# A hybrid decoder step on one core: cached keys laid out feature-major on the host, key transposes taken out

## The chip, the cores and the metric

The kernel runs on one core of one Trainium2 chip. The metric is the device time of one execution in microseconds (us).

## What is computed

One layer for 256 prompt tokens and 32 sample tokens (8 sequences of 4), 288 tokens together: a modulated RMSNorm, one input projection, three token mixers (a spatial gMLP, a gated DeltaNet, a sparse attention), one output projection. The change is in the sparse attention of the sample tokens, which looks at 2048 cached keys per sequence, held in 16 pages of 128 keys with 2 heads of 128 features:

```python
idx, valid = _indexer_topk(q_idx, w_idx, pos, kidx_all, top_k)        # 256 of 2052 keys per query
k_sel = jnp.where(is_past, cache_k[phys, off], _gather_rows(k, nidx))
v_sel = jnp.where(is_past, cache_v[phys, off], _gather_rows(v, nidx))
s = jnp.einsum('bthgd,btkhd->bthgk', q, k_sel) * C_HEAD ** -0.5
p = jax.nn.softmax(jnp.where(valid, s, -jnp.inf), axis=-1)
```

The kernel scores all cached keys and masks those that were not selected.

## The kernel before

**Order of work.** A planner (class Weaver) writes the program. Units of matrix product (tile `acc`: weight matrices split in two parts, 12 matmuls of 288 columns for each half of a 512 KB weight load) are listed by hand; between the steps of a unit, generators (the attention, the DeltaNet, and so on) put in their own stages whenever the planner's clock says that their inputs are there. So most stages are covered by `acc` matmuls, and each engine runs its instructions in the order in which the planner wrote them. The planner's clock uses costs of its own: 1.0 us of GpSimd for each DMA that GpSimd issues (line 193), 0.003 + 0.000416 us per column for an `acc` matmul, which is 0.123 us (line 119), and for data that GpSimd gathers 0.6 us, the bytes at 360 GB/s and 2.0 us until they can be read (lines 193 to 206).

**Forced waits.** `W.finish(...)` runs named generators to their end without any `acc` matmul between them. Before the last unit of each q, k or v group of the DeltaNet projection stands `end_prev` (lines 2285 to 2290): all causal convolutions (`CONV`) that have been started must be finished, and for the third q group (g = 2, kind 0) also `DN[0]`, the first of the four DeltaNet head groups. `DN[0]` starts when the sample attention is done (`X.g_smp.done`, line 1701).

**The sample attention.** `idx_sample_gen` builds gather indices from the page table, gathers and scores the indexer keys, sets `idx_done`, and goes on with `topk_gen`: 32 rounds of max and replace on VectorE, each followed by a small copy `LDn<-LU` on GpSimd. `sample_gen` runs in two halves `hf` of 4 sequences. In each half:

- 16 gathers of keys into `kraw` (two buffers). One gather fetches 128 rows of 4 KB, one per partition: 4 neighbouring keys, 2 heads, 128 features; 512 KB.
- two lanes, `qk_lane(0)` and `qk_lane(1)`, take them in turn. For each gather there are 8 transposes on TensorE into two PSUM banks (tile `kT`), two copies out of them (VectorE and ScalarE, tile `ktk`), 8 score matmuls for 32 query rows each (tile `S`, each of which is two instructions in the trace), and two copies of scores by ScalarE into `S`.
- then gathers of values (tile `vraw`, 2 KB rows, buffers shared with `kraw` and `kt`), the mask matmuls once top-k is done (`X.topk`), softmax, transposes `pT`, value matmuls `so`.

The gathers are indirect DMAs, issued from GpSimd's queue. In the same queue stand the `LDn` copies, the constants `Rm` and `segm`, and the convolution taps of the sample tokens (`cv`, `tap`, `SSG`). Every kernel instruction is recorded at line 74, the wrapper of the engines, so the views are read by tile names.

Of the kernel before, what the change touches and what calls it, by code (L numbers as in the profile page):

```python
# [12 lines left out]
I32 = mybir.dt.int32  # L13
# [6 lines left out]
P = 128  # L20
# [70 lines left out]
class Weaver:  # L91
# [195 lines left out]
    def bank(self, n=1):  # L287

        yield
        while not self.room(n):  # L290
            yield lambda: self.room(n)
        self.take(n)
# [88 lines left out]
def tile_hybrid_step(ctx: ExitStack, tc: tile.TileContext, I, O):  # L381
# [22 lines left out]
    def tl(pool, shape, name, bufs=1, dt=F32, tag=None):  # L404
        return W.tile(pools[pool][1], shape, dt, tag or name, name, bufs)
# [764 lines left out]
    def idx_sample_gen():  # L1170
# [4 lines left out]
        dma(ptB, bass.AP(tensor=pt.tensor, offset=pt.offset, ap=[[0, P], [1, P]]))  # L1175
        iof = tl("ap", [P, 16], "iof")
        G.iota(iof, pattern=[[1, 16]], base=0, channel_multiplier=0, allow_small_or_imprecise_dtypes=True)
        sub16 = tl("ap", [P, 1], "sub16")
        V.memset(sub16, 0.0)
        sv = tl("ap", [P, 4], "sv")  # L1180
        V.memset(sv, 16.0)

        for q in range(4):
            G.affine_select(sv[:, q:q + 1], sv[:, q:q + 1], pattern=[[0, 1]], compare_op=OP.is_ge, fill=0.0,
                            base=-32 * q - 16, channel_multiplier=1)
            G.affine_select(sv[:, q:q + 1], sv[:, q:q + 1], pattern=[[0, 1]], compare_op=OP.is_ge, fill=0.0,
                            base=32 * q + 31, channel_multiplier=-1)
        iop = tl("ap", [P, 2], "iop")
        G.iota(iop[:, 0:1], pattern=[[0, 1]], base=0, channel_multiplier=1, allow_small_or_imprecise_dtypes=True)
        m15 = tl("ap", [P, 16], "m15")  # L1190
# [3 lines left out]
        V.scalar_tensor_tensor(iop[:, 1:2], iop[:, 1:2], -8.0, iop[:, 0:1], op0=OP.mult, op1=OP.add)  # L1194
        V.tensor_scalar(iop[:, 1:2], iop[:, 1:2], 8.0, None, op0=OP.mult)

        ptm = pts[:, 384:448].rearrange("p (b j) -> p b j", j=16)
        G.memset(ptm, 0.0)
        for u in range(2):
            G.affine_select(ptm, ptm, pattern=[[-32, 4], [-1, 16]], compare_op=OP.not_equal, fill=1.0,  # L1200
                            base=-16 * u, channel_multiplier=1)
        ptj = pts[:, 448:464]
        G.affine_select(ptj, ones[:, 0:16], pattern=[[-8, 16]], compare_op=OP.is_ge, fill=0.0, base=0,
                        channel_multiplier=1)
        G.affine_select(ptj, ptj, pattern=[[8, 16]], compare_op=OP.is_ge, fill=0.0, base=7, channel_multiplier=-1)
        yield [ptB]
        V.tensor_reduce(sub16, sv, axis=AX.X, op=OP.max)
        ptf = tl("ap", [P, 3], "ptf")
        ptvf = tl("ap", [P, NB], "ptvf")
        V.tensor_copy(ptF, ptB)  # L1210
        V.tensor_tensor(ptT, ptF, ident, op=OP.mult)
        V.tensor_reduce(ptf[:, 0:1], ptT, axis=AX.X, op=OP.add)
        V.tensor_tensor(ptT.rearrange("p (h n) -> p h n", h=2), ptF.rearrange("p (h n) -> p h n", h=2),
                        pts[:, 384:448][:, None].to_broadcast([P, 2, 64]), op=OP.mult)
        V.tensor_reduce(ptf[:, 1:3], ptT.rearrange("p (h n) -> p h n", h=2), axis=AX.X, op=OP.add)
        V.tensor_tensor(ptT.rearrange("p (b j) -> p b j", j=16), ptF.rearrange("p (b j) -> p b j", j=16),
                        ptj[:, None].to_broadcast([P, NB, 16]), op=OP.mult)
        V.tensor_reduce(ptvf, ptT.rearrange("p (b j) -> p b j", j=16), axis=AX.X, op=OP.add)
        ix8 = tl("ap", [P, 8], "ix8", 1, I32)
        V.scalar_tensor_tensor(ix8, ptf[:, 0:1].to_broadcast([P, 8]), 8.0, iof[:, 0:8], op0=OP.mult, op1=OP.add)  # L1220
        X.ixk = tl("ap", [P, 2, 16], "ixk", 1, I32)
        for hf in range(2):
            V.tensor_scalar(ptf[:, 1 + hf:2 + hf], ptf[:, 1 + hf:2 + hf], 32.0, sub16, op0=OP.mult, op1=OP.add)
            V.tensor_scalar(X.ixk[:, hf], iof, ptf[:, 1 + hf:2 + hf], None, op0=OP.add)

        V.tensor_scalar(ptvf, ptvf, 64.0, iop[:, 1:2], op0=OP.mult, op1=OP.add)
        X.ixv = tl("ap", [P, NB, 8], "ixv", 1, I32)
# [203 lines left out]

    def sample_gen():
        yield lambda: hasattr(X, "qready")
        k_rows = I["cache_k"][0].rearrange("n (e l) h d -> (n e) (l h d)", e=32)
        v_rows = I["cache_v"][0].rearrange("n (e l) h d -> (n e) (l h d)", e=64)
        qS = X.qS
        yield lambda: hasattr(X, "idx_done")
        def gather_k(hf, s):
            raw = tl("ap", [P, 4, 256], "kraw", 2)
            G.indirect_dma_start(out=raw.rearrange("p l c -> p (l c)"), out_offset=None, in_=k_rows,  # L1440
                                 in_offset=bass.IndirectOffsetOnAxis(ap=X.ixk[:, hf, s:s + 1], axis=0))
            return raw

        def gather_v(hf, s):
# [14 lines left out]
        for hf in range(2):  # L1459

            S = tl("ap", [P, NK], "S", 1, tag="S")
            Sk = S[:, 0:2048].rearrange("p (c k) -> p c k", k=P)
            raws = [gather_k(hf, 0), gather_k(hf, 1)]

            def qk_lane(par):
                raw = raws[par]
                for s in range(par, 16, 2):
                    yield [raw]
                    yield from bank(2)
                    pk = [pr4("kT") for _ in range(2)]  # L1470
                    for kv in range(2):
                        for l in range(4):
                            T.transpose(pk[kv][:, l], raw[:, l, kv * HD:(kv + 1) * HD], ident)
                    if s + 2 < 16:
                        raw = gather_k(hf, s + 2)
                    yield [pk[1]]
                    kt = tl("ap", [P, 2, 4, P], "ktk", 2, tag="kt")
                    V.tensor_copy(kt[:, 0], pk[0])
                    A.copy(kt[:, 1], pk[1])
                    free(2)  # L1480
                    yield from bank()
                    ps = pr("S")
                    qk_mm(ps, P, hf, lambda kv, bb: kt[:, kv, :, 32 * bb:32 * bb + 32])
                    yield
                    dst = Sk[:, 4 * (s % 4):4 * (s % 4) + 4].rearrange("p l (j u w) -> p l w u j", u=2, w=4)[:, :, s // 4]
                    for u in range(2):
                        A.activation(dst[:, :, u], ps[:, 0:P].rearrange("p (l u j) -> p u l j", l=4, u=2)[:, u], AF.Copy,
                                     scale=HD ** -0.5)
                    free()

            ls = W.push(qk_lane(0), qk_lane(1), front=True)
            yield lambda: all(x.done for x in ls)
            raws = []
            raws += list(gather_v(hf, 0)) + list(gather_v(hf, 1))
            yield from bank()
# [921 lines left out]
    for i, (_, n, t0) in enumerate(xsrc):  # L2417
# [11 lines left out]
    close_pool("fp")  # L2429


_INS = ["x_prompt", "x_sample", "cache_k", "cache_v", "cache_kidx", "state_dn", "state_conv", "page_table",
        "c_prompt", "c_sample", "w_ada_t", "b_ada", "g_norm", "w_in_t", "w_in_c", "a_vnorm", "a_ws", "a_bs", "dn_conv_w",
        "dn_a_log", "dn_dt_bias", "dn_onorm", "w_out_t", "g_final"]
_OUTS = [((1, 256, 4096), "float32"), ((8, 4, 4096), "float32"),
# [6 lines left out]
def lay_out(inputs):  # L2442

    import numpy as np

    a = dict(inputs)
    w = np.asarray(a.pop("w_in"))[0]
    idx = np.concatenate([np.arange(c, c + 512) for c in GCOL])
    a["w_in_t"] = w[:, idx].reshape(16, 2, P, 29, 512).transpose(3, 0, 2, 1, 4)
    c = np.concatenate([w[:, C_KIWI:C_KIWI + 80], w[:, C_AB:C_AB + 32]], axis=1)  # L2450
    a["w_in_c"] = c.reshape(16, 2, P, 112).transpose(0, 2, 1, 3)
    a["w_out_t"] = np.asarray(a.pop("w_out"))[0].reshape(16, 2, P, 8, 512).transpose(3, 0, 2, 1, 4)
    w = np.asarray(a.pop("w_ada"))[0]
    blocks = []
    for k0, n in STEPS:
        x = w[:, :2 * D].reshape(n * 8, 4 // n, P, 2, D)[..., k0 * P:(k0 + n) * P]
        blocks.append(x.transpose(0, 2, 1, 3, 4).reshape(8 * n, P, 1024))
    for f in range(4):
        blocks.append(w[:, 2 * D + 1024 * f:2 * D + 1024 * f + 1024].reshape(KT, P, 1024))
    a["w_ada_t"] = np.concatenate(blocks)  # L2460
    return a
# [21 lines left out]
```

## Time and profile before

| | |
|---|---|
| median of 3 runs | 2645.76 us (2639.38 to 2648.55) |
| the profiled execution | 2644.57 us, span 2642.8 us |
| TensorE (PE) busy | 2531.5 us, 96% of the span |
| VectorE (DVE), ScalarE (ACT), GpSimd (POOL) busy | 62%, 40%, 19% |
| mean granted TensorE clock | 0.986 of full |

Matmuls overlap in the records, so a busy TensorE is not one at its peak; what one matmul costs is read from the distance between starts, and from the chain.

### The profile page before, as it was taken

How to read it: one execution, taken by the hardware profiler on the slowest of the kernel's cores; microseconds unless marked ns; L12 is line 12 of the kernel's file. 1: busy time of each engine (PE TensorE's matmuls, PEld its weight loads, DVE VectorE, ACT ScalarE, POOL GpSimd, SP SyncE). 2: the span in 40 equal slices, each digit the busy share in tenths (PEclk: the TensorE clock that was granted, in tenths of full speed). 3: DMA queues.
4: the chain of work that ended last, by engine and by line, in shares of the span. 5: the costliest groups of instructions: out<-in, count | busy, mean ns of one | idle time of the engine just before them, and what ended most of it. 6: DMA issues, size and time to landing. Idle time of an engine off the chain costs nothing.

```text
span 2642.8 us, 52171 instructions
## 1 busy us (share of the span) xinstructions
PE 2531.5 (96%) x19684; PEld 2237.9 (85%) x19684; DVE 1629.5 (62%) x3633; ACT 1064.3 (40%) x2440; POOL 495.5 (19%) x1137
## 2 busy tenths in 40 slices
PE   5999999999998999999999989999999999999997
PEld 2777878888897878877789969989989989999997
DVE  3377765555567777744457658568576667555554
ACT  3433233323244443334254444444444544444443
POOL 1000000000001042263542333443440210000000
PEclk9999999999999999999999999999999999999998
DMA  7998988888656477677767547567568465655564
GB/s 276 339 326 327 346 320 301 313 312 302 239 171 209 162 236 239 207 278 251 255 221 248 173 147 245 179 212 255 178 202 267 146 193 183 179 181 177 175 187 164
DMA packets 234964, 615.91 MB, mean 233 GB/s; under 512 B 38856, under 2 KB 92348, under 8 KB 234712
## 3 DMA queue, kind: packets, MB, share of 16 engines
q1 hardware_dynamic: 223672, 574.65, 64.6%
q0 software_dynamic: 11040, 37.92, 4.2%
q8 instruction: 155, 2.54, 0.4%
q14 instruction: 97, 0.79, 0.1%
HBM read 587.54 MB, written 24.95 MB: 232 GB/s over the span
## 4 chain that ended last, share of the span: by engine, by line
PE 85%; DMA 6%; DVE 3%; issue 2%; POOL 2%; ACT 1%; SPq 0%; another core or an unknown queue 0%; ACTq 0%; DVEq 0%; POOLq 0%
PE acc L74 68%; PE ada L74 7%; DMA kraw<-in_cache_k_dram,ixk 2%; DMA wa<-in_w_ada_t_dram 1%; PE Sup L74 1%; PE kT L74 1%; PE YP L74 1%; DVE wl L74 1%; DMA w<-in_w_in_t_dram 1%; PE v L74 1%; PE so L74 1%; PE gram L74 1%; PE o L74 1%; DMA prev<-in_state_conv_dram 0%; DMA vraw<-in_cache_v_dram,ixv 0%
## 5 line engine op out<-in xcount | busy, mean ns | idle before, releaser
L74 DVE TENSOR_TENSOR wl<-w,wh 128x512 fp32r<-128x512 f32 (+1 forms) x1216 | 803.0, 682 | 694.9 <-ACT wh L74 645.1
L74 ACT CAST wh<-w 128x512 fp32r<-128x512 f32 (+1 forms) x1216 | 714.3, 611 | 1173.3 <-PE acc L74 846.0
L74 PE MATMUL acc<-hH,wh 128*128 128x288 f32 (+1 forms) x3744 | 1159.7, 310 | 14.4 <-ACT hH L74 8.7
L74 PE MATMUL acc<-hH,wl 128*128 128x288 f32 (+1 forms) x3744 | 1108.7, 296 | 6.0 <-DVE wl L74 3.9
L74 PE MATMUL acc<-hL,wh 128*128 128x288 f32 (+1 forms) x3744 | 1107.8, 296 | 1.3 <-issue 0.9
L74 PEld LDWEIGHTS acc<-hH,wh 128*128 128x128 f32 (+1 forms) x3744 | 706.4, 189 | 175.6 <-ACT wh L74 90.2
L74 PEld LDWEIGHTS acc<-hH,wl 128*128 128x128 f32 (+1 forms) x3744 | 706.9, 189 | 9.7 <-DVE wl L74 7.6
L74 PEld LDWEIGHTS acc<-hL,wh 128*128 128x128 f32 (+1 forms) x3744 | 707.4, 189 | 4.4 <-issue 3.2
L74 PE MATMUL acc<-mL,wh 128*128 128x288 f32 x1024 | 302.4, 295 | 2.5 <-DVE mL L74 2.5
L74 PE MATMUL acc<-mH,wh 128*128 128x288 f32 x1024 | 304.3, 297 | 0.0
L74 PE MATMUL acc<-mH,wl 128*128 128x288 f32 x1024 | 302.8, 296 | 0.0
L74 PEld LDWEIGHTS acc<-mL,wh 128*128 128x128 f32 x1024 | 193.0, 188 | 2.7 <-DVE mL L74 2.7
L74 PEld LDWEIGHTS acc<-mH,wh 128*128 128x128 f32 x1024 | 192.9, 188 | 0.2
L74 PEld LDWEIGHTS acc<-mH,wl 128*128 128x128 f32 x1024 | 192.9, 188 | 0.0
L74 PE MATMUL ada<-wa,cT 128*32 128x512 f32 x1024 | 149.9, 619 | 17.6 <-DMA wa<-in_w_ada_t_dram 17.6
L74 DVE TENSOR_TENSOR zb<-zb,acc 128x288 f32<-128x288 f32 x160 | 70.6, 451 | 41.1 <-PE acc L74 40.4
L74 POOL TENSOR_TENSOR htmp<-yT,gaT 128x32 f32<-128x32 f32 x20 | 7.7, 387 | 449.9 <-DVE gaT L74 449.9
L74 POOL TENSOR_SCALAR frs<-frs 128x1 f32<-128x1 f32 (+1 forms) x3 | 0.9, 296 | 451.2 <-DVE frs L74 451.1
L74 POOL TENSOR_SCALAR tap<-xp,cwT 128x32 f32<-128x32 f32 x144 | 79.5, 552 | 0.1
L74 DVE TENSOR_TENSOR R<-R,R 128x248 f32<-128x248 f32 (+30 forms) x248 | 72.5, 292 | 10.8 <-DMA w<-in_w_in_t_dram 2.2
L74 DVE SCALAR_TENSOR_TENSOR cv<-xp,cwT,cv 128x256 f32<-128x256 f32 x144 | 70.3, 488 | 3.7
L74 POOL DMA_INDIRECT vraw<-in_cache_v_dram,ixv x64 | 65.2, 1019 | 31.2 <-issue 14.7
(462 smaller groups left out, 2350.5 us busy)
## 6 DMA issues: line engine op xcount, KB each, us to landing
w<-in_w_in_t_dram SPq DMA_DIRECT2D x464, 512.0 KB
wa<-in_w_ada_t_dram SPq DMA_DIRECT2D x256, 512.0 KB
w<-in_w_ada_t_dram SPq DMA_DIRECT2D x128, 512.0 KB
w<-in_w_out_t_dram SPq DMA_DIRECT2D x128, 512.0 KB
St<-in_state_dn_dram SPq DMA_DIRECT2D x16, 512.0 KB
out_dram<-St SPq DMA_DIRECT2D x16, 512.0 KB
X<-in_x_prompt_dram SPq DMA_DIRECT2D x8, 512.0 KB
XF<-in_x_prompt_dram SPq DMA_DIRECT2D x16, 256.0 KB
```

Of the source, the lines that this page charges most:

```text
L74: r = f(*a, **k)
```

## The change

The host hands over `cache_k_t`: the same keys as (page, feature, head, key). One gather now fetches one page with features on the partitions, 128 rows of 1 KB (2 heads, 128 keys), so keys come in as the score matmul wants them. The transposes `kT` and the copies `ktk` go. A half needs 64 gathers of 128 KB where it had 16 of 512 KB; they go into four buffers (`kraw` and `kt` in turn, 512 KB each, 4 gathers a buffer). The two lanes become one loop of 8 steps: a step waits for two buffers (8 gathers), runs 16 score matmuls into one PSUM bank, issues the 8 gathers of the step after the next, and ScalarE copies 256 columns with one instruction. The index for keys is one [128 x 128] table; the operations that built the old one go.

```diff
-        X.ixk = tl("ap", [P, 2, 16], "ixk", 1, I32)
-        for hf in range(2):
-            V.tensor_scalar(ptf[:, 1 + hf:2 + hf], ptf[:, 1 + hf:2 + hf], 32.0, sub16, op0=OP.mult, op1=OP.add)
-            V.tensor_scalar(X.ixk[:, hf], iof, ptf[:, 1 + hf:2 + hf], None, op0=OP.add)
+        X.ixk = tl("ap", [P, P], "ixk", 1, I32)
+        V.tensor_scalar(X.ixk, ptF, 128.0, iop[:, 0:1], op0=OP.mult, op1=OP.add)
...
-        k_rows = I["cache_k"][0].rearrange("n (e l) h d -> (n e) (l h d)", e=32)
+        k_rows = I["cache_k_t"].rearrange("n d h k -> (n d) (h k)")
...
-        def gather_k(hf, s):
-            raw = tl("ap", [P, 4, 256], "kraw", 2)
-            G.indirect_dma_start(out=raw.rearrange("p l c -> p (l c)"), out_offset=None, in_=k_rows,
-                                 in_offset=bass.IndirectOffsetOnAxis(ap=X.ixk[:, hf, s:s + 1], axis=0))
+        def gather_k(hf, j):
+            raw = tl("ap", [P, 4, 2, P], "kraw", 2, tag="kt" if j % 2 else "kraw")
+            for bb in range(4):
+                i = 16 * (4 * hf + bb) + j
+                G.indirect_dma_start(out=raw[:, bb].rearrange("p h k -> p (h k)"), out_offset=None, in_=k_rows,
+                                     in_offset=bass.IndirectOffsetOnAxis(ap=X.ixk[:, i:i + 1], axis=0))
             return raw
...
-            raws = [gather_k(hf, 0), gather_k(hf, 1)]
-            def qk_lane(par):
...
-            ls = W.push(qk_lane(0), qk_lane(1), front=True)
-            yield lambda: all(x.done for x in ls)
+            raws = [gather_k(hf, j) for j in range(4)]
+            for s in range(8):
+                two = [raws.pop(0), raws.pop(0)]
+                yield two
+                yield from bank()
+                ps = pr("S")
+                for jj in range(2):
+                    qk_mm(ps[:, jj * P:jj * P + P], P, hf, lambda kv, bb: two[jj][:, bb, kv])
+                if s < 6:
+                    raws += [gather_k(hf, 2 * s + 4), gather_k(hf, 2 * s + 5)]
+                yield
+                A.activation(Sk[:, :, 16 * s:16 * s + 16].rearrange("p c k -> p k c"),
+                             ps[:, 0:2 * P].rearrange("p (k c) -> p k c", c=16), AF.Copy, scale=HD ** -0.5)
+                free()
...
+    a["cache_k_t"] = np.asarray(a.pop("cache_k"))[0].transpose(0, 3, 2, 1)
```

Left out of the diff: in `idx_sample_gen` eight `affine_select` on `sv`, two on `ptm`, three memsets and three VectorE operations go.

## Rows read from the trace of the kernel before

**Rows 1.** The page's first part: the span, then an engine's busy time, its share and its instructions.

```profile
span 2642.8 us, 52171 instructions
PE 2531.5 (96%) x19684; PEld 2237.9 (85%) x19684; DVE 1629.5 (62%) x3633; ACT 1064.3 (40%) x2440; POOL 495.5 (19%) x1137
```

**Rows 2.** Busy time by stretch: us from:to, length, then PE, PEld, DVE, ACT, POOL busy (instructions), granted TensorE clock, share of the DMA engines, GB/s.

```profile
913.00:1003.00 90.00, 84.81 (x910) 72.62 (x908) 67.59 (x137) 38.77 (x96) 32.78 (x67) 0.98 0.67 222
1003.00:1090.00 87.00, 82.29 (x610) 75.90 (x607) 62.24 (x135) 31.48 (x64) 14.34 (x43) 1.00 0.74 243
...
1171.00:1240.00 69.00, 63.76 (x685) 56.16 (x681) 30.01 (x56) 29.14 (x72) 24.61 (x35) 1.00 0.76 264
...
1375.00:1400.00 25.00, 25.00 (x188) 22.88 (x187) 14.03 (x29) 10.53 (x27) 2.61 (x7) 1.00 1.01 336
1400.00:1520.00 120.00, 119.55 (x929) 112.12 (x928) 81.65 (x201) 53.70 (x136) 41.78 (x101) 1.00 0.61 200
1520.00:1563.00 43.00, 30.68 (x245) 20.57 (x245) 22.70 (x84) 16.68 (x72) 17.99 (x49) 0.88 0.31 88
1563.00:2000.00 437.00, 436.63 (x3464) 398.70 (x3463) 299.92 (x748) 203.92 (x570) 164.93 (x404) 1.00 0.68 220
```

**Rows 3.** Instructions of the tiles `kT`, `ktk` and `S` (min/median/max ns, first and last start, forms), and four pieces of the chain (start, us, what) with a group of transposes and one of score matmuls.

```profile
L74 PE MATMUL kT<-ident,kraw x256: 270/273/373, 935.8 to 1236.7; 128*128 128x128 f32 x128
L74 DVE COPY ktk<-kT x32: 680/684/693, 936.4 to 1236.6; 128x512 f32<-128x512 f32 x32
L74 ACT COPY ktk<-kT x32: 586/587/591, 936.8 to 1237.1; 128x512 f32<-128x512 f32 x32
L74 ACT ACTIVATE S<-S x64: 278/292/363, 939.1 to 1239.8; 128x64 f32<-128x64 f32 x64
```

```profile
937.59 0.87 PE kT L74 x8
938.46 0.57 PE S L74 x16
...
1236.14 0.87 PE kT L74 x8
...
1238.21 0.57 PE S L74 x16
```

**Rows 4.** Waits of TensorE in the first and in the second score stage: engine, what, on what: us in total, times, longest.

```profile
PE kT L74 <- DMA kraw<-in_cache_k_dram,ixk: 4.1, 3, 1.8
...
PE kT L74 <- DMA kraw<-in_cache_k_dram,ixk: 4.7, 4, 3.2
```

**Rows 5.** The gathers on GpSimd: key and value gathers by tile, and the first two and the last of eight value gathers in a row (start, us, what, idle before).

```profile
L74 POOL DMA_INDIRECT kraw<-in_cache_k_dram,ixk x32: 937/951/1473, 913.9 to 1230.0; - x32
L74 POOL DMA_INDIRECT vraw<-in_cache_v_dram,ixv x64: 942/948/1491, 1000.7 to 1310.4; - x64
...
1000.73 0.97 POOL L74 DMA_INDIRECT vraw<-in_cache_v_dram,ixv  x1 [0.53 <-PE acc L74]
1002.01 0.96 POOL L74 DMA_INDIRECT vraw<-in_cache_v_dram,ixv  x1 [0.31 <-issue]
...
1009.53 0.94 POOL L74 DMA_INDIRECT vraw<-in_cache_v_dram,ixv  x1 [0.30 <-issue]
```

**Rows 6.** GpSimd in the first score stage: the first and the second key gather, the constants, the first and the last `LDn` copy.

```profile
913.88 1.41 POOL L74 DMA_INDIRECT kraw<-in_cache_k_dram,ixk  x1 [8.45 <-PE qk L74]
925.44 0.95 POOL L74 DMA_INDIRECT kraw<-in_cache_k_dram,ixk  x1 [10.15 <-PE kxT L74]
926.39 0.33 POOL L74 MEMSET Rm<- 128x256 bf16 x1
926.79 6.08 POOL L74 TENSOR_SCALAR_AFFINE_SELECT Rm<-Rm 128x64 bf16<-128x64 bf16 x16
...
933.20 2.91 POOL L74 TENSOR_SCALAR_AFFINE_SELECT segm<-segm 128x128 f32<-128x128 f32 x7
...
940.92 0.20 POOL L74 COPY LDn<-LU 128x8 f32<-128x8 f32 x1
...
1047.50 0.19 POOL L74 COPY LDn<-LU 128x8 f32<-128x8 f32 x1 [3.01 <-DVE LU L74]
```

**Rows 7.** GpSimd in the second score stage: the first key gather, copies that wait for the convolution on VectorE, the last key gather.

```profile
1171.58 1.03 POOL L74 DMA_INDIRECT kraw<-in_cache_k_dram,ixk  x1 [0.23 <-issue]
...
1188.02 0.21 POOL L74 COPY SSG<-cv 128x32 f32<-128x32 f32 x1 [2.77 <-DVE cv L74]
...
1230.03 0.94 POOL L74 DMA_INDIRECT kraw<-in_cache_k_dram,ixk  x1 [5.45 <-DMA kraw<-in_cache_k_dram,ixk]
```

**Rows 8.** TensorE after a wait for keys: starts of single matmuls (start, us, what).

```profile
957.25 0.64 PE L74 MATMUL S<-ktk,qS 128*32 128x128 f32 x16
959.74 1.17 PE L74 MATMUL kT<-ident,kraw 128*128 128x128 f32 x8 [1.85 <-DMA kraw<-in_cache_k_dram,ixk]
...
961.18 0.44 PE L74 MATMUL acc<-hH,wl 128*128 128x288 f32 x1
961.42 0.44 PE L74 MATMUL acc<-hH,wh 128*128 128x288 f32 x1
```

**Rows 9.** Matmuls in order of time: the first mask matmul; the first DeltaNet transposes of `DN[0]`; around the forced wait for `DN[0]`.

```profile
1088.63 0.37 PE L74 MATMUL mask<-mneg,Rm 32*128 32x512 bf16 x1 [1.30 <-DVE mneg L74]
...
1329.25 1.03 PE L74 MATMUL qkT<-ident,cv 128*128 128x128 f32 x8
...
1520.61 0.49 PE L74 MATMUL sT<-ident,SSG 128*128 128x128 f32 x3
...
1562.69 0.38 PE L74 MATMUL acc<-hH,wh 128*128 128x288 f32 x1
```

More of the change, by code (lines that the diff above doesn't have):

```diff
@@ L1177, in idx_sample_gen @@
         G.iota(iof, pattern=[[1, 16]], base=0, channel_multiplier=0, allow_small_or_imprecise_dtypes=True)
[L1178 to L1187, printed above, removed]
         iop = tl("ap", [P, 2], "iop")
@@ L1195, in idx_sample_gen @@
         V.tensor_scalar(iop[:, 1:2], iop[:, 1:2], 8.0, None, op0=OP.mult)
[L1197 to L1201, printed above, removed]
         ptj = pts[:, 448:464]
@@ L1206, in idx_sample_gen @@
         yield [ptB]
-        V.tensor_reduce(sub16, sv, axis=AX.X, op=OP.max)
-        ptf = tl("ap", [P, 3], "ptf")
+        ptf = tl("ap", [P, 1], "ptf")
         ptvf = tl("ap", [P, NB], "ptvf")
@@ L1212, in idx_sample_gen @@
         V.tensor_reduce(ptf[:, 0:1], ptT, axis=AX.X, op=OP.add)
-        V.tensor_tensor(ptT.rearrange("p (h n) -> p h n", h=2), ptF.rearrange("p (h n) -> p h n", h=2),
-                        pts[:, 384:448][:, None].to_broadcast([P, 2, 64]), op=OP.mult)
-        V.tensor_reduce(ptf[:, 1:3], ptT.rearrange("p (h n) -> p h n", h=2), axis=AX.X, op=OP.add)
         V.tensor_tensor(ptT.rearrange("p (b j) -> p b j", j=16), ptF.rearrange("p (b j) -> p b j", j=16),
@@ L1462, in sample_gen @@
             Sk = S[:, 0:2048].rearrange("p (c k) -> p c k", k=P)
-            raws = [gather_k(hf, 0), gather_k(hf, 1)]
-            def qk_lane(par):
[L1466 to L1489, printed above, removed]
-            ls = W.push(qk_lane(0), qk_lane(1), front=True)
-            yield lambda: all(x.done for x in ls)
+            raws = [gather_k(hf, j) for j in range(4)]
[12 more added lines that the diff above has]
+                free()
             raws = []
@@ L2429, in tile_hybrid_step @@
     close_pool("fp")
-_INS = ["x_prompt", "x_sample", "cache_k", "cache_v", "cache_kidx", "state_dn", "state_conv", "page_table",
+_INS = ["x_prompt", "x_sample", "cache_k_t", "cache_v", "cache_kidx", "state_dn", "state_conv", "page_table",
         "c_prompt", "c_sample", "w_ada_t", "b_ada", "g_norm", "w_in_t", "w_in_c", "a_vnorm", "a_ws", "a_bs", "dn_conv_w",
```

## Prediction

> **What bounds the kernel now.** I read the page's first part for the busiest engine, the stretches for where that holds, the waits of TensorE in the two score stages, and then GpSimd's queue in order of time. The reader is to see three things.
>
> TensorE is the bound nearly everywhere: busy 96% of the span [rows 1], and 436.6 of 437 us after 1563 us [rows 2]. `acc` matmuls fill what the other stages leave. Work taken off TensorE is a gain one for one, as long as fill remains for the gaps.
>
> The one place where fill has run out is the stretch 1520 to 1563 us: no unit may go on until `DN[0]` is done (end_prev, third q group), TensorE is busy 30.7 of 43 us there and its granted clock falls to 0.88 [rows 2, 9]. So a second path runs below TensorE's: top-k (first mask matmul at 1088.6 us), second half of the scores, value stage, `DN[0]` from 1329 us on, the forced wait. Longer pieces on it, or less fill to cover it, come back there as idle time.
>
> In the score stages TensorE waits little for keys, 4.1 and 4.7 us [rows 4], and GpSimd is busy 32.8 of 90 and 24.6 of 69 us [rows 2].
>
> **The change part by part.**
>
> *Transposes, removed.* 256 of them, in 32 groups of 8. A record lasts 273 ns, but they overlap: a group takes 0.87 us in the chain, 0.109 us each [rows 3]. 32 x 0.87 = 27.8 us off TensorE, nothing in their place. The Trainium skill (TensorE: Matmul & The Clock Gate, Part 4) gives about 275 ns for such a transpose in a kernel; this trace's record agrees at 273 ns. By that figure 256 of them would be 70 us and the kernel would take 2575 us; the groups of the chain say 28, and they decide.
>
> *Score matmuls, the same.* 16 instructions per 128 keys and sequence group, 0.57 us a group [rows 3], as many as before; the operand becomes contiguous, which no row prices; I take nothing.
>
> *Copies, removed.* VectorE 32 x 0.684 = 21.9 us, ScalarE 32 x 0.587 = 18.8 us; ScalarE's 64 score copies of 64 columns (0.292 us) become 16 of 256. Between 64 columns at 0.292 and 512 at 0.587 us [rows 3] a straight line gives 0.42 us, so 18.7 us become 6.7. I cost these at nothing: both engines are below TensorE in the second stage. In the first, VectorE is busy 67.6 of 90 us [rows 2] and top-k's 32 rounds (940.9 to 1047.5 us, 3.3 us each [rows 6]) share it with the copies of the first half: 16 x 0.684 = 11 us may come off top-k, if `acc` splits don't take the place. It shortens the second path, not TensorE's.
>
> *Waits for keys of before, removed with the transposes:* 4.1 + 4.7 = 8.8 us [rows 4].
>
> *Gathers: 32 become 128.* GpSimd needs 0.95 us for a gather of 4 KB rows and 0.948 us for one of 2 KB rows, so the price is per gather, not per byte; eight in a row stand 1.26 us apart ((1009.53 - 1000.73) / 7) [rows 5]. I take this for 1 KB rows too. 64 a half: 80.6 us of queue, where 16 took 20. GpSimd becomes the pace of both score stages.
> First half: 16 gathers can go ahead of the rest, but the `kt` buffers and the second `kraw` are free only at about 925 us [rows 6], so these end near 936. Then come `Rm` and `segm` (about 11 us with gaps), 48 x 1.26 = 60 and some 25 `LDn` copies at 0.25 (6 us): the last keys near 1013 + 4. The planner counts 1.0 us a gather, 6.8 for the constants and 4.5 for the copies, 62 us with landing, and covers that with `acc` work that really takes 0.133 instead of 0.123 us, 9% more: 68 us. GpSimd needs 77: TensorE waits 9 us in all.
> Second half: 80.6 us, some 8 us of convolution taps in the same queue and 4 to land, 93 us, against a plan of 64 + 8 + 3 = 75, really 82: 11 us, and 2 for copies that first wait for VectorE (2.77 us at 1188 [rows 7]). Sum 22 us. Bounds: nothing, if units are slower than planned; 45, if lags of both stages double.
>
> *What is queued behind the gathers:* `LDn` copies, needed only after the 32 rounds, and convolution taps, which ScalarE's `cth` and then `end_prev`'s CONV wait for. A tap round now stands behind 8 gathers, 10 us; two heads of the second convolution group are left when the second stage begins, three such rounds each: some 60 us, done near 1235, and that group's successor ends its matmuls at about 1235 too. 0 to 10 us, I take 2.
>
> *Clock.* After 1.85 us of waiting the `acc` matmuls stood 0.24 us apart for 3.4 us [rows 8] before they were back at 0.133, some 1.6 us lost. The second stage kept a granted clock of 1.00 with a wait of 3.2 us in it [rows 2, 4]. Some 16 new, short ones: 0 to 10 us, I take 2.
>
> *Second path and forced wait.* The second score stage grows from 67 us (1171.6 to 1239) to about 96, of which the plan sees 17. Top-k gives perhaps 14 back. Fill ends 28 us earlier since TensorE has less to do. So about 31 us of `DN[0]` that were covered (the last heads before 1520 us) lose their cover. Uncovered they take about half, 16 us, of which 9 are TensorE's own work: 7 us of new idle time. Bounds 0 and 20. After 1563 us nothing differs.
>
> *DMA.* Bytes are the same. Stretches with 512-byte rows still reach 336 GB/s at a full share [rows 2], so rows of 1 KB cost little; keys ask for 128 KB per 1.26 us, 104 GB/s, below the 130 GB/s of before. Nothing.
>
> *Index building.* A handful of operations of 0.2 to 0.3 us near 810 us, under `acc` work: nothing, 2 us of the second path at most.
>
> Sum: -27.8 - 8.8 + 22 + 2 + 2 + 7 = -3.6 us. From the profiled 2644.57 us that is 2641.0 us; the median of before is 1.2 us higher than that execution.
>
> **The rivals.**
>
> *The gain comes through (chance 0.32).* The planner knows that gathers cost GpSimd time, starts 16 early and puts units between. For it: TensorE waits only 8.8 us now with two buffers in flight; there will be four. Against: 1.26 us against a planned 1.0, 128 times. No new waits and 7 us at the forced wait: 2644.6 - 36.6 + 7 = 2615 us.
>
> *GpSimd's queue decides, slower (0.27).* The place is the second score stage, the price 60 us more of queue than before. If TensorE's waits reach 45 us there and in the first stage, with 9 more for taps and clock, and 56 us of `DN[0]` instead of 31 lie bare (28 us, 17 of them work: 11): 2644.6 - 36.6 + 45 + 9 + 11 = 2673 us at the bad end, 2660 in its middle. It decides from the point where the new waits, taps and clock together pass 30 us (36.6 less 7); I count 26.
>
> *Transfers become late, not GpSimd (0.05, counted with slower).* Keys come in packets of 1 KB beside weights in packets of 4 KB. If the engines took turns packet by packet while both queues are full, keys would get a fifth, 67 of 336 GB/s [rows 2], and a half's 8.4 MB would take 125 us instead of 80: 2 x 45 more, less what the cover takes, near 2690 us. Against: the share was 0.67 and 0.76 [rows 2], so both queues are not full all the time. The Trainium skill (DMA: Bandwidth & Descriptors, Queues, rings and completion order) states such a turn by packets. No row here shows it by itself.
>
> *The nearly cancelled sum (0.36)* is my forecast, 2641 us, its own range 2632 to 2652.
>
> **How the numbers follow.** A measurement of this kernel tells about 0.3% (8 us) from no change. Faster: the first rival and a fifth of the forecast's cases, 0.40. Slower: 0.27 + 0.05, less the part of the second rival below 2654 us, 0.26. Same: 0.34. Likeliest is the nearly cancelled sum, 2641. Range for 8 in 10: 2614 to 2664, which cuts the best part of the first rival and the bad end of the others; its width is the bounds on the waits (0 to 45) and on the forced wait (0 to 20).
>
> **What would show it.** Right: no `kT` and `ktk`; 128 key gathers of about 0.95 us some 1.26 us apart; TensorE busy 28 us less; waits of `S` matmuls for `kraw` of about 20 us in all; the last key gather of the second half some 80 to 90 us behind the first; the forced wait for `DN[0]` longer than 42 us although it begins earlier. Wrong: gathers of 1 KB rows clearly cheaper or dearer than 0.95 us, top-k ending much earlier or held up by GpSimd, a forced wait for convolutions, or landings over 8 us.

## The result and the profile after

The changed kernel takes 2671.1 us (median of 4, 2667.7 to 2673.1) beside 2645.4 for the kernel before: ratio 1.0094, 95% interval 1.0072 to 1.0116. It is 25 us slower. The forecast was 2641 us with 2614 to 2664 as range; the time lies outside it, on the side of the second rival ("GpSimd's queue decides, slower", 2660 to 2673 us).

The page of after, first part, the two groups of gathers and the queue that carries them (for a group: count | busy us, mean ns | idle before, releaser; for a queue: packets, MB, share of the 16 engines):

```profile
span 2671.4 us, 51579 instructions
PE 2532.6 (95%) x19428; PEld 2229.6 (83%) x19428; DVE 1610.0 (60%) x3593; ACT 1042.6 (39%) x2360; POOL 582.8 (22%) x1222
...
q0 software_dynamic: 12576, 37.93, 4.4%
...
L74 POOL DMA_INDIRECT kraw<-in_cache_k_t_dram,ixk x128 | 129.9, 1015 | 47.8 <-issue 33.5
...
L74 POOL DMA_INDIRECT vraw<-in_cache_v_dram,ixv x64 | 65.4, 1022 | 37.6 <-PE so L74 18.5
```

256 instructions fewer on TensorE than in [rows 1], and its busy time is 1 us up: records overlap and grow longer at a lower granted clock (an `acc` record lasts 0.44 us behind the wait of [rows 8] and 0.29 in the row at 1506.54 us below), so this sum does not show the work that went. The stretches show more (columns as in [rows 2]: the first score stage, the end of top-k, the second score stage, the forced wait for `DN[0]`, behind it):

```profile
913.00:1003.00 90.00, 80.71 (x790) 69.80 (x789) 39.25 (x86) 28.39 (x58) 69.76 (x91) 0.92 0.70 235
1003.00:1110.00 107.00, 102.23 (x786) 93.92 (x786) 84.66 (x160) 40.22 (x81) 30.02 (x81) 0.98 0.71 237
1224.00:1320.00 96.00, 86.14 (x738) 71.80 (x731) 29.97 (x58) 29.73 (x62) 73.21 (x90) 0.88 0.66 222
1506.00:1600.00 94.00, 66.39 (x445) 49.71 (x447) 41.41 (x143) 32.47 (x139) 33.58 (x96) 0.80 0.20 57
1600.00:2000.00 400.00, 399.69 (x3187) 364.41 (x3180) 278.07 (x697) 185.61 (x522) 156.32 (x385) 1.00 0.66 216
```

Two things stand out against [rows 2]. The forced wait is 89 us long instead of 40. And in the first score stage VectorE is busy 39 us of 90 instead of 68: the copies that went are 11 us of that, and the rounds of top-k fell from 33 to 8 us there, since most of them run later (some other work took their place). The instructions of the tiles `LDn`, `mask` and `qkT` (min/median/max ns, first and last start):

```profile
L74 POOL COPY LDn<-LU x32: 185/190/249, 962.8 to 1105.5; 128x8 f32<-128x8 f32 x32
L74 PE MATMUL mask<-mneg,Rm x10: 185/384/386, 1153.1 to 1332.4; 32*128 32x512 bf16 x8, 32*128 32x32 bf16 x2
L74 PE MATMUL qkT<-ident,cv x64: 270/273/421, 1409.0 to 1996.1; 128*128 128x128 f32 x64
```

And in order of time the last `acc` matmul before the forced wait for `DN[0]` and the first one behind it:

```profile
1506.54 0.29 PE L74 MATMUL acc<-hH,wl 128*128 128x288 f32 x1
...
1595.88 0.38 PE L74 MATMUL acc<-hH,wh 128*128 128x288 f32 x1
```

Top-k's last copy is 58 us later than in [rows 6], the first mask matmul 64 us, the start of `DN[0]` 80 us, the end of the forced wait 33 us later than in [rows 9]; the whole kernel 28.6 us by span. GpSimd's queue in the first score stage shows how top-k lost its time (start, us, what):

```profile
961.85 0.94 POOL L74 DMA_INDIRECT kraw<-in_cache_k_t_dram,ixk  x1 [0.30 <-issue]
962.79 0.20 POOL L74 COPY LDn<-LU 128x8 f32<-128x8 f32 x1
963.16 1.44 POOL L74 DMA_INDIRECT kraw<-in_cache_k_t_dram,ixk  x1 [0.17 <-issue]
...
973.16 0.95 POOL L74 DMA_INDIRECT kraw<-in_cache_k_t_dram,ixk  x1 [0.30 <-issue]
974.10 0.20 POOL L74 COPY LDn<-LU 128x8 f32<-128x8 f32 x1
...
1004.40 0.95 POOL L74 DMA_INDIRECT kraw<-in_cache_k_t_dram,ixk  x1 [0.30 <-issue]
1005.35 0.20 POOL L74 COPY LDn<-LU 128x8 f32<-128x8 f32 x1
```

One `LDn` copy per 8 gathers, 10 to 11 us apart, where a round took 3.3 us before: five rounds done at 1005 us, when the last key gather of the half was issued.

The 80 us of `DN[0]` divide as follows. The second half's first key gather comes 53 us later than in [rows 7], at 1224.2 us, behind a first mask that is 64 us late. From there to the last score matmul it takes 94 us instead of 67 (1238.21 in [rows 3]), 27 us more. From there to `DN[0]` it takes 91 us in both kernels.

```profile
L74 PE MATMUL S<-kraw,qS x256: 272/273/423, 1242.2 to 1318.0; 128*32 128x128 f32 x128
```

### The profile page after: what moved, and what is told of

It reads as the page before. It is cut to its first block, busy times and chain, and to the rows that moved or that the text cites. A ratio compares the mean times of both kernels' runs of the same rounds, so it can differ in the third digit from the quotient of the medians.

```text
span 2671.4 us, 51579 instructions
## 1 busy us (share of the span) xinstructions
PE 2532.6 (95%) x19428; PEld 2229.6 (83%) x19428; DVE 1610.0 (60%) x3593; ACT 1042.6 (39%) x2360; POOL 582.8 (22%) x1222
## 3 DMA queue, kind: packets, MB, share of 16 engines
q0 software_dynamic: 12576, 37.93, 4.4%
## 5 line engine op out<-in xcount | busy, mean ns | idle before, releaser
L74 POOL DMA_INDIRECT kraw<-in_cache_k_t_dram,ixk x128 | 129.9, 1015 | 47.8 <-issue 33.5
```

The costliest lines, as they stand in the source:

```text
L74: r = f(*a, **k)
```

## The experiments

Four readings were tried against each other. **A**: the planner lets each round of top-k wait for the `LDn` copy of the round before; the copy stands behind 8 gathers, so the rounds are written out 10 us apart and the whole second path is late. **B**: TensorE's waits for keys in the score stages are the price. **C**: the removed transposes were worth little. **D**: it is the end of `DN[0]`, and so of the forced wait, that sets the time.

The table has one line for each profiled run: starts of the first and the last mask matmul and of the first transposes of `DN[0]`; the forced wait (last `acc` or `ada` matmul before it, first one behind it; a dash where no stretch over 6 us without them is left); the span; what of the span lies behind the wait; the ratio to the kernel before timed beside it. Spans are of the one profiled execution and stand up to 9 us off the run's median, so a price told by span is rough, and the ratio decides.

| kernel | mask first, last | `DN[0]` | forced wait | span | behind | ratio (95%) |
|---|---|---|---|---|---|---|
| before | 1088.6, 1258.5 | 1329.3 | 1522.8–1562.7 | 2642.8 | 1080.1 | 1 |
| after | 1153.1, 1332.4 | 1409.0 | 1506.5–1595.9 | 2671.4 | 1075.5 | 1.0094 (1.0072–1.0116) |
| e1_free_rounds | 1112.1, 1299.3 | 1367.9 | 1505.1–1577.2 | 2656.7 | 1079.5 | 1.0052 (1.0034–1.0071) |
| e1_ldn_act | 1119.5, 1316.3 | 1390.0 | 1496.4–1586.2 | 2662.8 | 1076.6 | 1.0089 (1.0072–1.0105) |
| e3_few_gathers | 1082.9, 1234.3 | 1304.1 | 1483.3–1530.8 | 2608.6 | 1077.8 | 0.9857 (0.9841–0.9873) |
| e4_before_late | 1188.8, 1350.7 | 1427.4 | 1499.2–1600.7 | 2681.5 | 1080.8 | 1.0141 (1.0124–1.0158) |
| e5_plan_before | 1050.3, 1208.8 | 1333.1 | – | 2650.7 | | 0.9990 (0.9975–1.0006) |
| e5_plan_after | 1108.4, 1296.7 | 1367.7 | 1542.8–1582.8 | 2661.2 | 1078.4 | 1.0053 (1.0032–1.0073) |
| e6_keys_by_sync | 1108.4, 1294.8 | 1366.4 | 1550.9–1592.9 | 2672.4 | 1079.5 | 1.0111 (1.0086–1.0136) |
| e7_gather_price | 1158.1, 1359.2 | 1433.8 | 1475.9–1591.1 | 2670.0 | 1078.9 | 1.0096 (1.0079–1.0113) |
| e8_few_late | 1140.9, 1288.1 | 1357.3 | 1463.2–1553.9 | 2630.8 | 1076.9 | 0.9916 (0.9894–0.9939) |
| e9_free_plan | 1056.7, 1233.1 | 1323.0 | – | 2640.1 | | 0.9955 (0.9929–0.9981) |
| e10_two_queues | 1065.8, 1218.4 | 1293.9 | – | 2603.5 | | 0.9845 (0.9822–0.9868) |
| e11_two_queues_plan | 1024.7, 1186.3 | 1307.9 | – | 2626.6 | | 0.9929 (0.9905–0.9954) |
| e12_few_first | 1084.0, 1301.4 | 1377.5 | 1510.5–1581.5 | 2658.7 | 1077.2 | 1.0023 (1.0010–1.0035) |
| e13_few_second | 1171.9, 1312.4 | 1391.8 | 1504.4–1594.5 | 2670.5 | 1076.0 | 1.0075 (1.0053–1.0098) |
| e14_before_free | 1081.3, 1243.5 | 1321.4 | – | 2634.3 | | 0.9928 (0.9907–0.9949) |
| e15_two_queues_bound | 1100.6, 1269.4 | 1339.2 | 1527.0–1568.7 | 2646.6 | 1077.9 | 0.9968 (0.9952–0.9984) |

In all thirteen runs with a forced wait, 1075.5 to 1080.8 us lie behind it, while its end moves over 70 us. So where the wait is bare (no `acc` matmul covers it) the kernel's time follows the end of the wait, and TensorE's own work and waits count only as far as they move that. That is reading D, and it holds in the kernel before too. It does not say by itself what moves that end, and it does not apply to the five runs without a bare wait, whose spans differ by 47 us; what sets their time is not worked out here.

**e1_free_rounds**

```diff
+            e = W.end
             G.tensor_copy(LD_[:, n], mx)
+            W.end = e
```

> The changed kernel, but the planner no longer lets a round of top-k wait for GpSimd's LDn copy of the round before (the copy stays where it is, on GpSimd; nothing on the chip needs it before the 32 rounds are over). Theory A (the rounds of top-k are written out behind the key gathers, so the first mask matmul comes at 1153 us instead of 1089, DN[0] starts 80 us late and its forced wait grows from 43 to about 90 us): first mask near 1090 us, forced wait ending near 1565 us, and some 20 to 25 us back, 2646 to 2652 us. Theory B (TensorE's waits for keys in the two score stages are the price, some 35 us of new idle time there): these waits stay, and so does the time, 2666 to 2673 us.

Measured 2658.0 us: some 11 us of the 25 come back by the ratios (1.0094 to 1.0052), less than A's 20 to 25, more than B's nothing. Top-k's copies in it:

```profile
L74 POOL COPY LDn<-LU x32: 181/191/647, 964.8 to 1062.9; 128x8 f32<-128x8 f32 x32
```

And TensorE's waits for keys in the first and in the second score stage (us in total, times, longest):

```profile
PE S L74 <- DMA kraw<-in_cache_k_t_dram,ixk: 8.8, 7, 2.7
...
PE S L74 <- DMA kraw<-in_cache_k_t_dram,ixk: 11.8, 10, 3.1
```

The last copy is 43 us earlier than in after with one mark of the planner changed, and the first mask matmul 41 us, still 23 us later than before. Nothing on the chip held the rounds: here VectorE starts the fifth round at 966.76 us, and the copies of the second to the fifth run 10 us behind it, in one go between two gathers.

```profile
966.76 0.72 DVE L74 MAX8 LU<-W 128x8 f32<-128x544 f32 x1
...
976.44 0.56 POOL L74 COPY LDn<-LU 128x8 f32<-128x8 f32 x4
```

The waits for keys are what they were (10.3 and 9.8 us in after, below). A's mechanism is shown; it is not the whole loss. Below, rounds with this mark are called freed, those without it bound.

**e1_ldn_act**

```diff
-            G.tensor_copy(LD_[:, n], mx)
+            A.copy(LD_[:, n], mx)
```

> The changed kernel with the 31 LDn copies of top-k on ScalarE instead of GpSimd: nothing of top-k's rounds stands in GpSimd's queue, in the plan or on the chip. Theory A: as in the kernel with the freed rounds, first mask near 1090 us and 2646 to 2652 us. If it gains more than that one, the copies' own place in GpSimd's queue counts too (31 x 0.25 us, up to 8 us). Theory B: 2664 to 2673 us.

Measured 2666.2 us, a miss: the first mask matmul came 34 us earlier than in after, the last only 16, and the time is the same as after's within the intervals. By the code the rounds now wait in the plan for ScalarE's copy instead. Against e1_free_rounds, `DN[0]` is 22 us later, most of it behind the scores: from the last score matmul (1290 us) to `DN[0]` it takes 100 us, where e1_free_rounds takes 83. Why is not shown. Moving the copy is no substitute for freeing the round.

**e3_few_gathers** (one gather of 4 KB rows for four of 1 KB)

> The changed kernel with 32 key gathers of 4 KB rows in place of 128 of 1 KB: the same bytes into the same buffers, but each gather takes 32 rows of 4 features, so the scores are made from the wrong keys; all other work is as in the changed kernel. It shows what the change would be without the 96 extra gathers. Theories A and B both put the whole loss on the extra gathers: transposes and old waits gone (-36.6 us) and no new ones, 2605 to 2618 us. Rival C (the transposes were worth little, since acc work only moved up into their place until DN[0] is waited for): 2630 to 2645 us.

Measured 2605.7 us, 1.4% under before. C falls: without the extra gathers the change gives about the 36.6 us of transposes and waits that the sum had for it. Here TensorE's busy time does fall, by 32 us against [rows 1]:

```profile
PE 2499.8 (96%) x19428; PEld 2213.8 (85%) x19428; DVE 1608.9 (62%) x3594; ACT 1042.9 (40%) x2360; POOL 494.5 (19%) x1126
```

The run holds all of the change but the gathers (copies that went and four buffers too), so it does not price the transposes alone; by D its gain is a forced wait that ends 32 us earlier. 62.8 us of span between this kernel and after are the price of 96 gathers: the last `acc` matmul before the wait comes 23 us later in after (TensorE waits 20.2 us for keys there and 4.5 here), and the wait is 42 us longer. So B holds for a part.

**e4_before_late and e8_few_late** (`yield from W.pause(64.0)`, and 45.0, ahead of the 32 rounds)

> The kernel before, its 32 rounds of top-k begun 64 us later by the planner's clock, nothing else changed: theory A's delay by itself. Theory A: first mask near 1150 us, DN[0] some 64 us later, forced wait for it ending near 1590 us; 20 to 27 us slower, 2665 to 2672 us. Theory B: the cover takes most of it, 2645 to 2652 us.

> The kernel with 32 key gathers of 4 KB rows (scores from the wrong keys, as said there) with its rounds of top-k begun 45 us later by the planner's clock, which should bring the first mask matmul from 1083 to about 1150 us, as late as in the changed kernel, without its waits for keys. It gives the price of a late top-k alone, beside 2605.7 us. Theory A/D (0.4 us for 1 us of the second path): 2627 to 2637 us; what is then left to 2671 us, some 35 to 45 us, is the keys' own. If a late top-k were all: 2655 us or more. If the keys were all: 2605 to 2615 us.

Measured 2680.8 us, above A's forecast, and 2626.3 us. The pause delayed the first mask of before by 100 us, not by the 64 of the planner's clock, and cost 38.7 us of span: 0.39 us for 1. In the kernel with few gathers 58 us of delay cost 22 us by span, 16 by the ratios. A late top-k alone makes the kernel slower, with 2.6 us of waits for keys in e8, so B is not the whole either. Its price is well under 1 for 1, and with it goes a faster `DN[0]` (from its first transposes to the end of the wait 233 us in before, 227 with few gathers, 197 with few and late, 187 in after); that it is faster because it shares TensorE with less `acc` work is likely, and not tested.

**e12_few_first and e13_few_second** (`if hf == 0`, or `1`, one gather of 4 KB rows for four)

> The changed kernel with 16 key gathers of 4 KB rows in the first half of the scores (made from the wrong keys) and 64 of 1 KB in the second, as in the changed kernel. Top-k has no long queue before it; what is left is the price of the second half's 81 us of gathers. If the price is first of all top-k's order and the first stage: 2610 to 2620 us. If the second stage's pace weighs as much, being on the second path: 2625 to 2640 us. The two halves together make up 65 us between 2605.7 and 2671 us.

> The other way round: 64 gathers of 1 KB rows in the first half, as in the changed kernel, and 16 of 4 KB in the second (its scores from the wrong keys). Top-k stands behind the gathers, first mask near 1153 us; 16 to 22 us for that (the late top-k alone), and some 13 us of TensorE's waits in the first stage: 2635 to 2645 us. If the halves add up, this and the one before are together 65 us above 2605.7.

Measured 2656.4 and 2669.5 us, both above their forecasts: by the ratios 44 and 58 us above few gathers, 102 together where the whole change loses 63. The halves do not add up, and the expectation that they would was wrong. The second half's key gathers and score matmuls, with few gathers and in e12:

```profile
L74 POOL DMA_INDIRECT kraw<-in_cache_k_t_dram,ixk x16: 939/947/1325, 1168.1 to 1212.3; - x16
L74 PE MATMUL S<-kraw,qS x256: 272/273/297, 1176.9 to 1220.4; 128*32 128x128 f32 x128
...
L74 POOL DMA_INDIRECT kraw<-in_cache_k_t_dram,ixk x64: 942/946/1468, 1169.6 to 1270.6; - x64
L74 PE MATMUL S<-kraw,qS x256: 269/273/423, 1181.6 to 1277.8; 128*32 128x128 f32 x128
```

In e12 top-k is as early as with few gathers, and yet the last mask comes 67 us later: the second score stage alone takes 108 us instead of 52, at GpSimd's pace. In e13 that stage takes 53 us, but it begins 78 us later, behind a first mask that is 89 us later, later than in after. The forced wait grows from 47 us with few gathers to 71 and 90; in after, with both halves slow, it is 89. Beside the kernel before, e12 is 6 us slower and e13 20 us: the slow first half, with the late top-k in it, costs more than the slow second.

**e5_plan_before, e5_plan_after, e9_free_plan**

```diff
-PLAN = {"p1": [..., "zb2", "zb3"], "attn": ["za0", "za1"], "dn3": []}
+PLAN = {"p1": [..., "zb2"], "attn": ["za0", "za1", "zb3"], "dn3": []}
```

> The kernel before with one z group (zb3, 384 acc matmuls at 0.133 us, 51 us of TensorE) moved from ahead of the second path's start to behind it: the same work, but index scores, top-k, scores and DN[0] all begin 51 us earlier, with 51 us more of acc work to cover them before the forced wait for DN[0]. Theory D (every kernel's end is the end of DN[0] plus some 1118 us, so what comes late on the second path is paid, about 0.4 us for 1 us as in the delayed kernel before): the forced wait of 43 us shrinks, 10 to 20 us gained, 2622 to 2633 us. Theory B (TensorE's waits in the score stages decide): no change, 2638 to 2648 us.

> The changed kernel with the same z group moved in the same way. Theory D: its forced wait is longer, so the same 51 us are worth more here, 20 to 30 us, 2640 to 2652 us. Theory B: the waits for keys are not touched, 2664 to 2673 us.

> The changed kernel with the freed rounds of top-k and the moved z group together. Each alone gave 12 to 13 us. If both work on one thing, the lateness of the second path: less than their sum, 2648 to 2655 us. If on different ones: 2643 to 2648 us.

With the second path begun 36 and 39 us earlier (first key gather), the forced wait went from 89 to 40 us in the changed kernel, worth 11 us, and vanished in the kernel before, worth nothing: its first mask came 38 us earlier, its `DN[0]` not (1333 against 1329 us). What held it shows in the trace (the last value matmuls, the last transposes of a convolution, `DN[0]`):

```profile
1278.40 0.63 PE L74 MATMUL so<-vrep,pnT 32*32 32x256 f32 x8
...
1330.69 0.60 PE L74 MATMUL tailT<-ident,tail 128*27 128x128 f32 x4
...
1333.12 0.60 PE L74 MATMUL qkT<-ident,cv 128*128 128x128 f32 x4
```

The attention was done 54 us before `DN[0]` began; in before that distance is 7 us. By the code `DN[0]` also waits for the convolutions of its head group, and the moved z group now stands ahead of the units that feed them. TensorE was also busy 94.8 instead of 99.8 us from 600 to 700 us. Both gains that D forecast were too large, and for the kernel before the time is the one that B gave, though not for B's reason. The "1118 us" of D's first forecast is not borne out: 1080 us lie behind the wait in before. With the freed rounds on top (2636.9 us) the wait is gone and the changed kernel passes the kernel before, by more than the two gains added: a miss to the good side.

**e6_keys_by_sync**

```diff
-                G.indirect_dma_start(out=raw[:, bb]..., in_=k_rows, in_offset=...)
+                pg = nc.sync.value_load(X.ptI[0:1, i:i + 1], min_val=0, max_val=NPOOL - 1)
+                nc.sync.dma_start(raw[:, bb]..., I["cache_k_t"][bass.ds(pg, 1)]...)
```

> The changed kernel with its 128 key transfers issued by SyncE as ordinary transfers of one page (128 features x 256, rows of 1 KB), the page number read into a register; GpSimd gathers no keys. Scores need no transposes, as in the changed kernel. If the price of the change is GpSimd's 96 extra gathers (theories A and B alike), it goes: 2605 to 2620 us as with 32 gathers. Rival E (the transfers of 1 KB rows or the many transfers are dear wherever they are issued; reading a register and waiting for a buffer now holds up the weights in SyncE's queue): 2640 us or more.

Measured 2673.7 us, rival E. SyncE took 1.12 us for a page (median distance of two issues), hardly less than GpSimd, and it is the queue that issues the weights. TensorE's waits from 900 to 1400 us:

```profile
PE S L75 <- DMA kraw<-in_cache_k_t_dram: 28.3, 41, 1.3
PE acc L75 <- ACT wh L75: 16.9, 4, 8.9
```

More waits for keys than in after (20.2), and new ones for split weights, 16.9 us, where e10 below has 5.6. `DN[0]` starts 43 us earlier than in after, but the last `acc` matmul before the wait comes 44 us later, at 1550.9 us, and it ends only 3 us earlier: here the loss lies ahead of the forced wait. So 64 transfers a half cost as much in SyncE's queue as in GpSimd's, in part by another way. How much of it is the packets of 1 KB that SyncE's transfers move as (last section) is not shown.

**e7_gather_price** (`1.0` to `1.26` in `note_dma`)

> The changed kernel with the planner told 1.26 us for an issue on GpSimd instead of 1.0, as the gathers really stand apart; the order alone changes. Theory B (the plan's lag of 0.26 us a gather makes TensorE wait): waits for keys fall by some 15 us and so does the time, 2652 to 2660 us. Theory A: top-k's rounds are put still further apart in the plan and the second path later, 2668 to 2680 us.

Measured 2669.2 us, after's time. An honest price per gather does not help: TensorE waits 19.9 us for keys, as in after, so B's cure did not take, and the forced wait, 115 us, is the longest of all.

**e10_two_queues, e11_two_queues_plan, e14_before_free, e15_two_queues_bound** (of four pages two by each of the two calls above; freed rounds in all but the last)

> The changed kernel with freed rounds, and of the four key transfers of a page position two on GpSimd as now and two on SyncE with the page number read into a register: 32 gathers of 1.26 us and 32 SyncE transfers of 1.06 us a half, side by side, 40 us of queue in place of 81. If the pace of one queue is what the score stages wait for: waits and second path shrink together, 2615 to 2635 us. If what holds the keys is the landing of 1 KB rows or the order of SyncE's queue behind weights: 2650 us or more.

> The same with the moved z group. If the forced wait for DN[0] has still idle time in the kernel with two queues, 5 to 15 us less than that one; if the second path is no longer late there, nothing or a few us more, as in the kernel before.

> The kernel before with top-k's rounds freed from GpSimd's LDn copies in the plan, as a control: is that a gain of its own, whatever the keys' layout? Before, only 16 gathers stand in GpSimd's queue beside the 32 rounds and a round took 3.3 us; 2636 to 2646 us. 2630 us or less would say that much of the two-queue kernel's gain is not the layout's.

> The two-queue kernel without the freed rounds. GpSimd's queue holds 4 gathers between two copies in place of 8, so the rounds stand some 5 us apart in the first stage: first mask 15 to 40 us later than 1066 us, 2608 to 2622 us. If the order of top-k is a fault only of the long queue: 2604 to 2608 us.

e10, which gathers every key as after does, takes 2605.8 us, ratio 0.9845: 41 us under the kernel before, better than forecast. Its two queues of keys:

```profile
L75 POOL DMA_INDIRECT kraw<-in_cache_k_t_dram,ixk x64: 942/952/1452, 902.7 to 1199.2; - x64
L1429 SPq DMA_DIRECT2D kraw<-in_cache_k_t_dram x64: 337/338/444, 917.4 to 1195.5; - x64
```

The second score stage, and the stretch where before had its forced wait (columns as in [rows 2]):

```profile
1150.00:1212.00 62.00, 56.70 (x586) 48.83 (x586) 21.58 (x46) 20.84 (x38) 47.00 (x61) 0.94 0.88 289
...
1520.00:1563.00 43.00, 43.00 (x323) 39.79 (x322) 32.82 (x74) 17.88 (x42) 14.37 (x32) 1.00 0.85 273
```

The second score stage is back to about 60 us, TensorE is busy all of 43 us, and `DN[0]` starts 35 us earlier than in before. The Trainium skill (Perfetto Trace Analysis, DMA Optimizations) says that balancing DMAs over the engines that can issue them may help where descriptor generation is the bottleneck. The runs with bound rounds agree: 1.0094 with all keys on GpSimd (after), 1.0111 with all on SyncE (e6), 0.9968 with both (e15).

e14, the control, gains more than forecast: 2629.4 us, ratio 0.9928, so the freed rounds are a gain of their own, 19 us without the new layout. e15, the layout with two queues and bound rounds, takes 2640.3 us, far above its forecast, ratio 0.9968: 8 us under before. Together they give 41 us, more than 19 and 8, so the layout with two queues is worth 8 us beside the kernel before and 22 beside e14. With either alone `DN[0]` starts 27 and 45 us later than in e10, and in e15 42 us of the forced wait are left. e11 is 22 us slower than e10, against the forecast: `DN[0]` starts 14 us later there, but no bare wait is left, and TensorE is busy 92.0 us from 600 to 700 us where e10 has 99.8. The rest of the 22 us is not accounted for.

## Why the prediction was wrong

**What bounds the kernel.** It was read that fill runs out before 1563 us and that a second path runs below TensorE's. It was then said that work off TensorE is a gain one for one "as long as fill remains", and the sum was made of TensorE's time. But with a forced wait of 40 us, fill had not remained; the table shows that where it is bare the end of that wait sets the time. The frame should have been the second path, stage by stage.

**Transposes and old waits, -36.6 us.** Right in size: e3_few_gathers gives 34 us by span, 38 by its ratio, and its TensorE is busy 32 us less. That it comes out so closely is in part luck, since the sum was one of TensorE's time and the gain passes through a forced wait that ends earlier.

**Gathers, 0.95 us busy and 1.26 us apart, also for 1 KB rows.** Right: 0.946 us at the median and mostly 1.25 apart in the queue's rows above, with some that take up to 1.44.

```profile
L74 POOL DMA_INDIRECT kraw<-in_cache_k_t_dram,ixk x128: 942/946/1442, 908.9 to 1314.5; - x128
```

The bytes cost nothing new: q0 holds 4.4% of the engines with 12,576 packets; the median key gather landed 4.7 us after issue. The third rival, late transfers, did not come about, and its premise, that keys come in packets of 1 KB, was wrong. The packets of before, after and e10:

```profile
DMA packets 234964, 615.91 MB, mean 233 GB/s; under 512 B 38856, under 2 KB 92348, under 8 KB 234712
...
DMA packets 236497, 615.87 MB, mean 231 GB/s; under 512 B 40392, under 2 KB 93884, under 8 KB 236248
...
DMA packets 242644, 615.90 MB, mean 237 GB/s; under 512 B 40392, under 2 KB 102076, under 8 KB 242392
```

From 512 B to 2 KB there are 53,492 packets in before and in after. The 96 further gathers added 1536 packets under 512 B, 16 each, and none of 1 KB; from 2 to 8 KB there are 142,364 packets in both, so the rows moved in packets of 4096 bytes, as before. Only SyncE's 64 transfers of a page in e10 add packets of 1 KB, 8192, one for each row.

**New waits for keys, 22 us (9 and 13).** Right in size, the two stages again in order of time:

```profile
PE S L74 <- DMA kraw<-in_cache_k_t_dram,ixk: 10.3, 9, 4.0
...
PE S L74 <- DMA kraw<-in_cache_k_t_dram,ixk: 9.8, 9, 3.3
```

20.1 us, and the second half's stage is 96 us long (first key gather 1224.2, `Sn` out at 1320.4), as forecast. That it was right helped little, since most of the loss is counted elsewhere. Waits for values stood in no term: TensorE waits 10.5 us for `vraw` from 900 to 1400 us in after and 2.9 in before.

**Queued behind the gathers: "`LDn` copies, needed only after the 32 rounds".** This is the step that failed. It is true of the data and of the semaphores; it is not true of the program. The generator yields behind the copy, and the planner takes its next turn only when the copy is done by its clock. The code shows it, with the `yield` right behind the copy; no row of before does, where 16 gathers stood in that queue and not 64. Beside this step stood "Top-k gives perhaps 14 back", where the prediction's own part on the copies had 11; top-k gave 64 us the other way. e1_free_rounds, with nothing changed but that mark, gives back 41 us of lateness and about 11 us of time. It stays 14 us above before by its ratio, with a forced wait 32 us longer where the rule for it had 16: this step is the largest miss on the second path (the second score stage begins 53 us late, of the 80 us of `DN[0]`), and not the whole of the time.

**Forced wait, 7 us.** The rule (31 us lose their cover, half of it new) got a wrong input: by its own terms, 29 us more of score stage and 14 back from top-k, `DN[0]` would start 15 us later; it started 80 us later. The stage was right (27 us more measured), top-k was not. The wait began 16 us earlier and ended 33 us later, 49 us longer.

**Clock, 2 us; taps and convolutions, 2 us.** The granted clock was 0.92 and 0.88 in the two score stages, against 0.98 and 1.00: at most 6% of 90 and 12% of 96 us, 17 us, part of it idle anyway; what it cost is not shown, and 2 is likely too little. In the stretch of the forced wait it was 0.80, against 0.88 in [rows 2], which no term had. Of the convolutions no forced wait is seen: six other stretches from 900 to 1500 us have no `acc` for 6 to 13 us, and in each TensorE does score or value matmuls and waits for keys or values.

**The rivals.** The second one named one of the two places, the second score stage, and nearly the right time, 2673 us, with two wrong terms: waits of 45 us (20 measured) and 28 us more of bare wait, 11 of them new idle time (49 us longer measured). That the time agrees is luck. It had no part for top-k, though "top-k held up by GpSimd" stood among the signs that would make the forecast wrong.

What stays open: how the 63 us between few gathers and after divide over the two halves. Each alone costs 44 to 58 us by the ratios, so no split of the sum has a meaning here.

## What to carry to other kernels

When an edit lengthens an in-order queue, list every instruction that shares it, and for each ask not only who needs its result on the chip but what the program's order, or the planner that wrote it, makes wait for it. Where a profile shows a bare wait, count on the path that ends it and not on the busiest engine: work saved on that engine shows only once the wait is covered. And an edit that trades work on one engine for issues on another is best tried with two queues to issue from: with bound rounds the same layout lost 25 us from one queue and gained 8 from two; with freed rounds it lost 14 from one and gained 41 from two, of which 19 come without the layout.

## What the hardware showed that was not expected

A transfer with its page number read into a register costs SyncE 0.27 us for the read, 0.15 us for the address and 0.34 us for the issue; in a row they stand 1.12 us apart in e6, not the 1.06 that the expectation for e10 took. The Trainium skill (DMA: Bandwidth & Descriptors, Latency and other measured facts) gives about 600 ns as the floor of a `tensor_load`. In this trace the record of that read lasts 268 ns at the median and 262 at the least, so this case does not show that floor:

```profile
L1423 SPq TENSOR_LOAD <-ixk x128: 262/268/637, 929.1 to 1268.1; - x128
L1423 SPq FUSED_REGOPS  x128: 152/152/192, 929.8 to 1268.4; - x128
L1424 SPq DMA_DIRECT2D kraw<-in_cache_k_t_dram x128: 337/338/837, 930.5 to 1268.8; - x128
```

An indirect gather costs GpSimd the same 0.94 to 0.95 us at the median for rows of 1, 2 and 4 KB. The rows of one page lie next to each other, and gathered by GpSimd rows of 1 KB moved in packets of 4096 bytes; the same page moved by SyncE went in packets of 1 KB. ScalarE's copy of 128x256 scores into strided places took 634 ns, more than the 587 ns of a 128x512 copy in [rows 3] and the 0.42 us that a straight line gave.
